# A decoder layer on one core: first pair's q and k projection at the head, p's projection beside the last retention pair, retention output as [tokens, d]

## The chip, the core and the metric

The kernel runs on one core of a Trainium2 chip. The core has TensorE (matrix products, PE in the profile, with its weight loads as PEld), VectorE (DVE), ScalarE (ACT), GpSimd (POOL) and SyncE (SP, which here only issues DMAs). ACT and POOL issue some DMAs too. Each engine takes its instructions in the order of the program that a scheduler has laid out at build time. The metric is device time in microseconds, median of several runs; lower is better.

## What is computed

One decoder layer on 512 tokens of width 2048, all in float32. Cut to what matters here:

```python
h = rms_norm(x, g_mix)
aq, ak, av, rq, rk, rv, rg = split(h @ w_in)                 # seven times 1024 columns
aq = rotate(rms_norm(aq per head, q_norm)); ak likewise      # 8 heads of 128
a_out = moba_attention(aq, ak, av)                           # 2 blocks of 256: plain causal attention here
r = retention(rotate(rq), rotate(rk) * 128**-0.5, rv)        # 8 heads, decay per head
r = r * rsqrt(mean(r * r, over the head) + 1e-6) * g_ret
r_out = silu(rg) * r
x += concat(a_out, r_out) @ w_o
x += (silu(rms_norm(x) @ w_gate) * (rms_norm(x) @ w_up)) @ w_down
x += (p @ w_ple_proj) * sigmoid(rms_norm(x) @ w_ple_gate + b)
```

`p` is a second input of 512 tokens by 256; its product with `w_ple_proj` depends on nothing else.

## The kernel before, in words

Every float32 operand is split into a high part H (float32r) and a low rest L, and a product is three passes: H·H, H·L, L·H (`mm3`, lines 62 to 64). `split` makes H with an ACT copy (line 54) and L with a DVE subtraction (line 55). A weight unit is 256 rows by 512 columns, 512 KB in one DMA on SP; its split is one ACT and one DVE instruction of 128x1024. All large products but the q and k projections go through a seven-product scheme (`Group`, products "1", "5", "6", "3", "7", "2", "4"): four quarters of a weight matrix are added on DVE (line 70), and sums of activation quarters, the factors, are kept as tiles s1, s5 and so on. PSUM banks of the scheme are X, Y and Z, two tiles each.

The program has these stages.

1. **Head.** Ten bf16 products on zeros; then four steps `Plain`, one for each 512 columns of `w_pp`: 24 products of p with a weight unit into `tp`, ACT copies, stores to DRAM (`ppd`). Beside them `first_factors` loads sixteen 128x512 chunks of transposed x on SP (line 428), scales them on ACT (line 429), splits them into `h`, and makes the factors s5, s6, s3, s7 from each pair of chunks. Then three groups of 336 products: the values of attention, the values of retention, and the gates. x is also read row by row for the sum of squares (lines 494 to 496).
2. **Gates.** `gates` applies silu, transposes the result with TensorE (32 transposes of 128x128, line 304), copies it on ACT and stores it as [d, tokens] in `sgd`.
3. **Head pairs.** Eight times: a pair of heads. `qk_attn(i)` (four attention pairs) or `qk_ret(i)` (four retention pairs) projects q and k of the pair: 8 weight units of 24 products into four PSUM tiles `acc`, 192 products. `attend` or `retain` then handles the two heads one after the other, and `factors` writes factors of the pair's output, through four buffers `o`, to DRAM (`s_mix`). In program order the projection of pair i+1 stands after the heads of pair i, and the scheduler interleaves the two. The evacuation of `qk_attn` takes DVE, ACT and POOL work for each of four token blocks before the next pair can use its `acc` tiles. The evacuation of `qk_ret` copies each `acc` tile to `zr`, swaps its halves with two DMAs on ACT's queue into `mr`, and multiplies with tables on DVE (lines 699 to 709); `zr` and `mr` share four buffers, so q of the two heads goes first and k waits for buffers.
4. **retain.** Scores of four key blocks (12 products), times decay on DVE, split into PH and PL; `weighted` gives o as [d, tokens] in 12 products with the values as the stationary operand. The norm over d runs over partitions: the squares are split, summed by a product with ones (`rms_of`, line 584), the diagonal is picked out on DVE, POOL takes the power, and `over_partitions` spreads the result with four transposes (line 85).
5. **Change to w_o.** When the last projection has read `h`, the tiles s1, s5, s6, s3 of the next stage take its place. `back` fills them from DRAM with DMAs on POOL's queue, pairs 0 to 5 first; the last pairs, and s7, s2, s4, follow. No projection is left beside the last pair.
6. **w_o, gate and up, down, ple gate.** Groups of the seven-product scheme to the end, untouched by the change.

Of the kernel before, what the change touches and what calls it, by code (L numbers as in the profile page):

```python
# [14 lines left out]
ALU = mybir.AluOpType  # L15
# [18 lines left out]
def layer_kernel(ctx, tc, x, xT, pT, g_mix, wqk, w_vg, qk_norm, g_ret, w_ow, g_ffn,  # L34
# [80 lines left out]
    sgd = dram.tile([P, 8, T], F32, name="sg")  # L115
# [266 lines left out]
    raws = []  # L382
    for k in range(2):
        raw = ev_tile("v", name="praw")
        nc.sync.dma_start(raw, pT[k * P:(k + 1) * P, :])
        raws.append(raw)
    pTH = []
    for k in range(2):
        pTH.append([ev_tile("e1" if k == 0 else "e5", name="pT", dt=F32R) for _ in range(2)])
        split(*pTH[k], raws[k])  # L390

    class Plain:

        def __init__(self, n):
            self.n = n
            self.raw = rawq.tile([P, 2, T], F32, name="raw", tag="c")
            nc.sync.dma_start(self.raw, w_pp[n])
            steps.append((self, "p", 0))
# [4 lines left out]
        def extract(self, p, u):  # L403
            self.wh = wq.tile([P, 2, T], F32R, name="wh", tag="wh")
            self.wl = wq.tile([P, 2, T], F32R, name="wl", tag="wl")
            split(self.wh, self.wl, self.raw)

        def multiply(self, p, u):
            for b in range(NB):
                o = tp_p.tile([P, T], F32, name="tp", tag="tp")  # L410
                at = slice(b * P, (b + 1) * P)
                for c in range(2):
                    mm3(o, pTH[c][0][:, at], pTH[c][1][:, at], self.wh[:, c, :], self.wl[:, c, :],
                        c == 0, c == 1)
                if b % 2 == 0:
                    t = rawq.tile([P, 2, T], F32, name="pp", tag="bd")
                nc.scalar.activation(t[:, b % 2], o, AF.Copy)
                nc.sync.dma_start(ppd[b][:, self.n], t[:, b % 2])

    for u in range(NS):  # L420
        Plain(u)

    def first_factors(k):

        a = []
        for c in (2 * k, 2 * k + 1):
            t = ev_tile("o", 4, name="x")
            nc.sync.dma_start(t, xT[c * P:(c + 1) * P, :])
            nc.scalar.activation(t, t, AF.Copy, scale=gm[:, c:c + 1])
            a.append(t)  # L430
        for c in range(2):
            split(h[:, 2 * k + c, 0, :], h[:, 2 * k + c, 1, :], a[c])
# [23 lines left out]
    def gates():  # L456
        got = {}

        def finish(th, nh, b, part, _):
            tb = 2 * th + b  # L460
            s = ev_tile("o", 4, name="sg") if (th, nh) == (0, 0) else part
            nc.scalar.activation(s, part, AF.Silu, scale=rstd[0][:, tb:tb + 1])
            got[tb, nh] = s
            if len([k for k in got if k[1] == nh]) == NB:
                def turn(k):
                    t = ev_tile("o", 4, name="A")
                    nc.scalar.activation(t, chunk_of(lambda b: got[b, nh], k), AF.Copy)
                    nc.sync.dma_start(sgd[:, 4 * nh + k], t)
                for k in range(4):
                    later(1 + k // 2, lambda k=k: turn(k))  # L470
# [4 lines left out]
    for u in range(4):  # L475
        groups[0].load("11", u)
# [6 lines left out]
    def beside(i):  # L483

        for k in {-2: [0], -1: [1], 0: [2, 3], 1: [4, 5], 2: [6], 3: [7]}.get(i, []):
            first_factors(k)
        if i == 4:
            for q in ("12", "22"):
                for u in range(4):
                    groups[0].load(q, u)  # L490
        if 4 <= i < 20:
            b, s = divmod(i - 4, NS)
# [4 lines left out]
        elif i == 20:  # L497
# [60 lines left out]
    ones = ap.tile([P, P], F32R, name="ones", tag="ones")  # L558
# [373 lines left out]
```

## Time and profile before

| | us |
|---|---|
| median of three runs | 2471.4 |
| lowest and highest run | 2466.14, 2471.67 |
| the profiled execution | 2465.03 |
| its span in the trace | 2463.3 |

The profile is of one execution. Its page gives the busy time of each engine, the span in 40 slices of 61.6 us, the chain of work that ended last, and the costliest groups of instructions. The trace answers finer questions: busy time and count of instructions in any stretch, an engine's instructions in order of time, and what each waited for. A busy TensorE is not a TensorE at its peak, since products are pipelined: the number of products in a stretch says more than the busy time.

### The profile page before, as it was taken

The page shows a single profiled execution, that of the slowest core. Times are in us where ns is not written, and L with a number is a line of the kernel's source. Part 1 is how long each engine was busy: PE and PEld are TensorE (multiplying, and loading weights), DVE is VectorE, ACT ScalarE, POOL GpSimd, SP SyncE. Part 2 cuts the span into 40 slices and gives each one's busy share as a digit, 9 for nine tenths or more (in the row PEclk, how much of TensorE's full clock was granted, in tenths as well). Part 3 has the DMA queues.
Part 4 walks back from the last instruction along what each step waited for, and adds up shares of the span by engine and source line. Part 5 has one row for each costly group of instructions (what it writes and reads, how often), then busy time and mean ns, then how long its engine had stood idle before and what let it go on. Part 6 is the DMA issues. An engine that isn't in the chain of part 4 may idle for free.

```text
span 2463.3 us, 29311 instructions
## 1 busy us (share of the span) xinstructions
PE 2347.9 (95%) x10454; PEld 1914.3 (78%) x10454; DVE 1965.7 (80%) x2624; ACT 1192.9 (48%) x1811; POOL 89.0 (4%) x77
## 2 busy tenths in 40 slices
PE   7899999998994999999999999999999999999898
PEld 5678888777773787788888888888877878888677
DVE  7788556776666799898889888898879787789897
ACT  7645434444332456455445554555444433446543
POOL 0000021220000100200000000000000000000000
PEclk8999999999996999999999999999999999999999
DMA  7544643335455569443564445543595676767763
GB/s 270 168 157 167 193 128 109 117 120 167 155 168 190 208 216 355 145 142 123 167 192 147 136 130 178 188 144 131 171 383 191 244 301 203 276 247 240 267 211 120
DMA packets 163667, 465.71 MB, mean 189 GB/s; under 512 B 18496, under 2 KB 27072, under 8 KB 158144
## 3 DMA queue, kind: packets, MB, share of 16 engines
q1 hardware_dynamic: 159184, 444.95, 53.4%
q0 software_dynamic: 1632, 14.68, 1.6%
q10 hardware_dynamic: 2704, 4.20, 0.7%
q8 instruction: 82, 1.34, 0.2%
q14 instruction: 65, 0.53, 0.1%
HBM read 353.14 MB, written 106.43 MB: 187 GB/s over the span
## 4 chain that ended last, share of the span: by engine, by line
PE 74%; DVE 11%; DMA 9%; issue 3%; ACT 3%; SPq 0%; POOL 0%; ACTq 0%; DVEq 0%; POOLq 0%
PE Y L62 8%; PE Y L63 8%; PE Y L64 8%; PE Z L63 6%; PE Z L64 6%; PE Z L62 5%; PE X L63 5%; PE X L64 5%; PE X L62 5%; PE acc L62 4%; PE acc L63 4%; PE acc L64 4%; DVE wl L55 4%; DVE raw L70 3%; DMA h<-o 2%
## 5 line engine op out<-in xcount | busy, mean ns | idle before, releaser
L54 ACT ACTIVATE wh<-raw 128x1024 fp32r<-128x1024 f32 x726 | 767.4, 1059 | 828.4 <-PE Y L64 274.1
L55 DVE TENSOR_TENSOR wl<-raw,wh 128x1024 fp32r<-128x1024 f32 x726 | 883.7, 1222 | 299.1 <-ACT wh L54 295.1
L70 DVE TENSOR_TENSOR raw<-raw 128x1024 f32<-128x1024 f32 x376 | 453.4, 1218 | 32.1 <-DMA raw<-in_w_gu 11.5
L63 PE MATMUL Y<-wl,s 128*128 128x512 f32 x1080 | 425.6, 394 | 3.7 <-DVE wl L55 3.6
L64 PE MATMUL Y<-wh,s 128*128 128x512 f32 x1080 | 421.6, 390 | 0.0
L62 PE MATMUL Y<-wh,s 128*128 128x512 f32 x1080 | 379.0, 391 | 10.0 <-ACT wh L54 10.0
L63 PE MATMUL Z<-wl,s 128*128 128x512 f32 x752 | 297.6, 396 | 5.3 <-DVE wl L55 5.3
L64 PE MATMUL Z<-wh,s 128*128 128x512 f32 x752 | 293.7, 391 | 0.8 <-DVE s L55 0.8
L62 PE MATMUL Z<-wh,s 128*128 128x512 f32 x752 | 266.5, 394 | 3.1 <-DMA s<-h 2.2
L63 PE MATMUL X<-wl,s 128*128 128x512 f32 x656 | 258.3, 394 | 4.7 <-DVE wl L55 4.5
L64 PE MATMUL X<-wh,s 128*128 128x512 f32 x656 | 256.6, 391 | 0.0
L62 PEld LDWEIGHTS Y<-wh,s 128*128 128x128 f32 x1080 | 201.9, 188 | 56.9 <-ACT wh L54 15.2
L63 PEld LDWEIGHTS Y<-wl,s 128*128 128x128 f32 x1080 | 203.2, 188 | 49.3 <-DVE wl L55 8.0
L64 PEld LDWEIGHTS Y<-wh,s 128*128 128x128 f32 x1080 | 203.2, 188 | 41.0
L62 PE MATMUL X<-wh,s 128*128 128x512 f32 x656 | 231.6, 393 | 3.6 <-ACT wh L54 3.6
L63 PEld LDWEIGHTS Z<-wl,s 128*128 128x128 f32 x752 | 142.2, 189 | 38.5 <-DVE wl L55 9.6
L62 PEld LDWEIGHTS Z<-wh,s 128*128 128x128 f32 x752 | 141.0, 189 | 34.0 <-ACT wh L54 2.5
L64 PEld LDWEIGHTS Z<-wh,s 128*128 128x128 f32 x752 | 142.1, 189 | 29.6 <-DVE s L55 1.2
L63 PEld LDWEIGHTS X<-wl,s 128*128 128x128 f32 x656 | 123.8, 189 | 34.0 <-DVE wl L55 8.3
L62 PEld LDWEIGHTS X<-wh,s 128*128 128x128 f32 x656 | 123.3, 189 | 31.8 <-ACT wh L54 6.2
L64 PEld LDWEIGHTS X<-wh,s 128*128 128x128 f32 x656 | 123.9, 189 | 25.5
L62 PE MATMUL acc<-h,wh 128*128 128x512 f32 x256 | 101.9, 398 | 6.2 <-ACT zr L699 5.4
(200 smaller groups left out, 2844.1 us busy)
## 6 DMA issues: line engine op xcount, KB each, us to landing
raw<-in_w_gu SPq DMA_DIRECT2D x176, 512.0 KB, 4.3
raw<-in_w_dn SPq DMA_DIRECT2D x88, 512.0 KB, 5.8
a<-o SPq DMA_DIRECT2D x154, 256.0 KB, 2.8
raw<-in_wqk SPq DMA_DIRECT2D x64, 512.0 KB, 3.5
s<-a SPq DMA_DIRECT2D x14, 2048.0 KB, 11.0
raw<-in_w_vg SPq DMA_DIRECT2D x48, 512.0 KB, 5.1
raw<-in_w_ow SPq DMA_DIRECT2D x32, 512.0 KB, 5.6
xin<-x SPq DMA_DIRECT2D x64, 256.0 KB, 5.8
```

The source lines that it names most:

```text
L54: nc.scalar.activation(H, src, AF.Copy)
L55: nc.vector.tensor_tensor(L, src, H.bitcast(F32), op=ALU.subtract)
L62: nc.tensor.matmul(o, aH, bH, start=start, stop=False, skip_group_check=goes_on)
L63: nc.tensor.matmul(o, aH, bL, start=False, stop=False, skip_group_check=goes_on)
L64: nc.tensor.matmul(o, aL, bH, start=False, stop=stop, skip_group_check=goes_on)
L70: nc.vector.tensor_tensor(o, a, b, op=ALU.add)
```

## The change

First, `Plain` is now the q and k projection of attention pair 0: eight steps of 24 products that read `h` straight from its chunks into the banks Y and Z; the result goes to DRAM (`zd`) and is loaded back as `z0` when the pair's evacuation runs. `first_factors` is made in a second pass that loads x's chunks again. Second, p's projection stands after the last head pair. Third, the gates stay [tokens, d]: no transposes. Fourth, `retain` makes o as [tokens, d] with PH and PL as the stationary operand and the two parts of the values side by side as 256 columns, 20 products; the norm is then along the free axis, and the result is turned by four transposes at the end. Fifth, `back` is issued on SP, in pieces of two pairs, at the start of the last pair, and that pair's factors for "1", "5", "6", "3" go straight into the tiles.

```diff
     class Plain:
-        def __init__(self, n):
-            self.n = n
-            self.raw = rawq.tile([P, 2, T], F32, name="raw", tag="c")
-            nc.sync.dma_start(self.raw, w_pp[n])
-            steps.append((self, "p", 0))
+        def __init__(self):
+            self.raw, self.w = {}, {}
+            steps.extend((self, "q", u) for u in range(NC // 2))
+
+        def load(self, u):
+            self.raw[u] = rawq.tile([P, 2, T], F32, name="raw", tag="l1" if u < 4 else "c")
+            nc.sync.dma_start(self.raw[u], wqk[0, u])
...
         def multiply(self, p, u):
+            if u == 0:
+                self.acc = [pools["chain"].tile([P, T], F32, name=k, tag=k) for k in ("Y0", "Y1", "Z0", "Z1")]
+            wh, wl = self.w.pop(u)
             for b in range(NB):
-                o = tp_p.tile([P, T], F32, name="tp", tag="tp")
                 at = slice(b * P, (b + 1) * P)
                 for c in range(2):
-                    mm3(o, pTH[c][0][:, at], pTH[c][1][:, at], self.wh[:, c, :], self.wl[:, c, :],
-                        c == 0, c == 1)
...
+                    k = 2 * u + c
+                    mm3(self.acc[b], h[:, k, 0, at], h[:, k, 1, at], wh[:, c, :], wl[:, c, :], k == 0, k == NC - 1)
+            if u == NC // 2 - 1:
+                later(1, self.evac)
+
+        def evac(self):
+            for b in range(NB):
+                t = ev_tile("o", 4, name="z0")
+                nc.scalar.activation(t, self.acc[b], AF.Copy)
+                nc.sync.dma_start(zd[b], t)
...
     def beside(i):
-        for k in {-2: [0], -1: [1], 0: [2, 3], 1: [4, 5], 2: [6], 3: [7]}.get(i, []):
-            first_factors(k)
...
+        if -2 <= i < NC // 2 - 2:
+            for k in (2 * i + 4, 2 * i + 5):
+                t = h_chunk(k)
+                split(h[:, k, 0, :], h[:, k, 1, :], t)
+            first.load(i + 2)
+        if 3 <= i < 3 + NC // 2:
+            first_factors(i - 3)
...
+        if i == 0:
+            for b in range(NB):
+                t = rm_tile("z0")
+                nc.sync.dma_start(t, zd[b])
+                evac(b, t)
+        else:
+            rows([wqk[i, u] for u in range(NC // 2)], evac)
...
-        o = weighted(v, (PH, PL), j)
+        hd = slice(j * HD, (j + 1) * HD)
+        r = rp_tile("r", (P, NB, HD))
+        ms = stat.tile([P, NB], F32, name="ms")
+        for half in range(2):
+            o = at_p.tile([P, 2, 2, HD], F32, name="at", tag="at")
+            for qb in (2 * half, 2 * half + 1):
+                for kb in range(qb + 1):
+                    at = slice(384 * kb + qb * P, 384 * kb + (qb + 1) * P)
+                    nc.tensor.matmul(o[:, qb % 2], PH[:, at], v[:, kb, :, hd], start=kb == 0, stop=False)
+                    nc.tensor.matmul(o[:, qb % 2], PL[:, at], v[:, kb, :, hd], start=False, stop=kb == qb)
+            both = slice(2 * half, 2 * half + 2)
+            nc.scalar.activation(r[:, both], o[:, :, 0], AF.Copy)
+            plus(r[:, both], r[:, both], o[:, :, 1])
...
+        for qb in range(NB):
+            nc.scalar.activation(sq[:, qb * P:(qb + 1) * P], r[:, qb], AF.Square, accum_out=ms[:, qb:qb + 1])
+        nc.vector.tensor_scalar(ms, ms, 1.0 / HD, EPS, op0=ALU.mult, op1=ALU.add)
         rs = stat.tile([P, NB], F32, name="rs")
-        rms_of(sq, [rm_tile("sqs", dt=F32R) for _ in range(2)], sq, HD, rs)
-        nc.vector.tensor_tensor(r, over_partitions(rs), r, op=ALU.mult)
-        return r
+        power(rs, ms, NB)
...
     def back(p, pairs):
-        nc.gpsimd.dma_start(s_o[p][:, pairs].bitcast(F32), s_mix[p][:, pairs].bitcast(F32))
+        nc.sync.dma_start(s_o[p][:, pairs].bitcast(F32), s_mix[p][:, pairs].bitcast(F32))
...
+        if i + 1 == 2 * NPAIR:
+            h_ctx.close()
...
+            for u in range(3):
+                for p in "156":
+                    back(p, slice(2 * u, 2 * u + 2))
+            for p in "156":
+                back(p, slice(6, 7))
+            back("3", slice(0, 7))
...
+    for k in range(2):
+        raw = rm_tile("praw")
+        nc.sync.dma_start(raw, pT[k * P:(k + 1) * P, :])
+        both = ap.tile([P, 2, T], F32R, name="pT", tag="rope" if k == 0 else "pT")
...
+    for n in range(NS):
+        wh, wl = weights(w_pp[n])
+        accs = [acc_p.tile([P, T], F32, name="acc", tag="acc") for _ in range(NB)]
```

The order that the scheduler makes of it differs at three places. On SP at the start of the program, before:

```order
L385 DMA praw<-in_pT 128x512 x2
L397 DMA raw<-in_w_pp 128x1024 x4
L204 DMA raw<-in_w_vg 128x1024 x4
L478 DMA ident<-in_ident_c 128x128
```

and now (in_xT is transposed x, in_wqk the weights of q and k, in_w_vg those of values and gates):

```order
L422 DMA x<-in_xT 128x512 x2
L390 DMA raw<-in_wqk 128x1024
L422 DMA x<-in_xT 128x512
L390 DMA raw<-in_wqk 128x1024 x3
L422 DMA x<-in_xT 128x512
L390 DMA raw<-in_wqk 128x1024 x2
L422 DMA x<-in_xT 128x512
L204 DMA raw<-in_w_vg 128x1024
L422 DMA x<-in_xT 128x512
L204 DMA raw<-in_w_vg 128x1024 x3
L422 DMA x<-in_xT 128x512
```

Chunks of x, weights of q and k, and weights of the values now alternate, and the twelve weight units of the first group stand among the chunks that the projection needs.

On PE at the end of the projection of attention pair 1, which in both programs is followed by that of pair 2 (`acc`; `at` with qkH are scores, `at` with PH are the weighted values, `tp` with pt and z are transposes). Before:

```order
L64 MATMUL acc<-wh,h 128x512
L62 MATMUL at<-qkH 128x256 x2
L63 MATMUL at<-qkL,qkH 128x256
L64 MATMUL at<-qkH,qkL 128x256
L63 MATMUL at<-qkL,qkH 128x256
L64 MATMUL at<-qkH,qkL 128x256
L62 MATMUL acc<-wh,h 128x512
```

and now:

```order
L64 MATMUL acc<-wh,h 128x512
L665 MATMUL tp<-ident,pt 128x128 x7
L62 MATMUL at<-PH,v 128x512
L640 MATMUL tp<-ident,z 128x128 x4
L63 MATMUL at<-PL,v 128x512
L64 MATMUL at<-PH,v 128x512
L62 MATMUL at<-PH,v 128x384
L63 MATMUL at<-PL,v 128x384
L64 MATMUL at<-PH,v 128x384
L62 MATMUL at<-PH,v 128x256
```

The projection ends earlier against the attention of pair 0: the last transposes and the weighted values of its first head now stand behind it, with no product of a projection between them.

On PE around the last retention pair (line 738 turns the output of the pair before; the scores of four key blocks, 12 products, and the 20 products of lines 722 and 723 of the first head stand between the two pieces shown). Before, after the last projection product:

```order
L584 MATMUL tp<-sqs,ones 128x512 x2
L85 MATMUL tp<-ident,rs 128x128 x4
L62 MATMUL at<-qkH 128x512
L63 MATMUL at<-qkL,qkH 128x512
L62 MATMUL at<-qkH 128x384
```

and now:

```order
L738 MATMUL tp<-ident,r 128x128 x4
L62 MATMUL at<-qkH 128x512
L63 MATMUL at<-qkL,qkH 128x512
L62 MATMUL at<-qkH 128x384
```

```order
L64 MATMUL at<-qkH,qkL 128x512
L62 MATMUL acc<-wh,pT 128x512
L63 MATMUL acc<-wl,pT 128x512
L62 MATMUL acc<-wh,pT 128x512
L63 MATMUL acc<-wl,pT 128x512
```

p's 96 products stand behind the first head's scores and weighted values and the first scores of the second head; none stands ahead of them.

The reload, before, on POOL's queue (s are the tiles of the next stage, 3072 columns are 1.5 MB):

```order
L747 DMA s_6454<-mix_86 128x3072
L747 DMA s_6455<-mix_87 128x3072
L747 DMA s_6456<-mix_88 128x3072
L747 DMA s_6457<-mix_89 128x3072
L747 DMA s_6454<-mix_86 128x512
```

and now on SP's, from the last of the first ten pieces on:

```order
L746 DMA s_6346<-mix_86 128x512
L204 DMA raw<-in_w_ow 128x1024
L176 DMA mix_87<-o 128x512
L176 DMA mix_88<-o 128x512
L176 DMA mix_89<-o 128x512
L176 DMA mix_90<-o 128x512
L746 DMA s_6347<-mix_87 128x512
L176 DMA mix_91<-o 128x512
L746 DMA s_6348<-mix_88 128x512
L176 DMA mix_92<-o 128x512
L746 DMA s_6349<-mix_89 128x3584
L778 DMA praw<-in_pT 128x512 x2
```

Nine pieces of 512 KB and one of 256 KB stand ahead of the stores of the factors (`mix<-o`), and the load of p stands behind all of it.

## Rows read from the trace of the kernel before

**Rows 1.** The page: busy time by engine, then TensorE and its granted clock in 40 slices.

```profile
PE 2347.9 (95%) x10454; PEld 1914.3 (78%) x10454; DVE 1965.7 (80%) x2624; ACT 1192.9 (48%) x1811; POOL 89.0 (4%) x77
...
PE   7899999998994999999999999999999999999898
...
PEclk8999999999996999999999999999999999999999
```

**Rows 2.** Stretches: length, busy time (instructions) by engine, granted clock, DMA share, GB/s.

```profile
0.00:40.00 40.00, 33.78 (x124) 23.37 (x124) 22.12 (x39) 29.94 (x51) 0.20 (x4) 0.96 0.97 345
40.00:80.00 40.00, 28.49 (x86) 19.62 (x87) 39.50 (x68) 25.00 (x48) 0.00 (x0) 0.79 0.31 98
80.00:160.00 80.00, 75.11 (x320) 59.08 (x320) 60.78 (x67) 46.11 (x74) 1.39 (x1) 1.00 0.61 207
160.00:220.00 60.00, 60.00 (x266) 49.69 (x265) 46.47 (x48) 29.56 (x32) 0.00 (x0) 1.00 0.60 195
440.00:460.00 20.00, 16.76 (x77) 13.27 (x76) 15.36 (x31) 9.30 (x43) 7.35 (x8) 0.91 0.20 67
760.00:780.00 20.00, 1.62 (x5) 0.90 (x5) 10.08 (x19) 2.81 (x6) 1.03 (x1) 0.51 1.01 362
780.00:800.00 20.00, 7.29 (x20) 5.83 (x21) 10.69 (x20) 5.37 (x11) 1.15 (x2) 0.50 0.45 153
800.00:820.00 20.00, 16.71 (x71) 13.61 (x71) 12.73 (x21) 7.61 (x13) 1.64 (x2) 0.88 0.27 79
```

**Rows 3.** TensorE in order of time: start, duration, line, tiles [idle before, releaser].

```profile
755.12 0.40 PE L64 MATMUL acc<-h,wl 128*128 128x512 f32 x1
...
791.39 0.80 PE L62 MATMUL at<-qkH 128*128 128x512 f32 x1 [26.34 <-ACT qkH L54]
...
801.44 0.28 PE L63 MATMUL at<-PL,v 128*128 128x256 f32 x1
801.56 0.28 PE L64 MATMUL at<-PH,v 128*128 128x256 f32 x1
...
811.84 0.39 PE L62 MATMUL X<-wh,s 128*128 128x512 f32 x1
```

**Rows 4.** The other engines there: POOL's reload, DVE on a swap, ACT on a store.

```profile
755.84 2.94 POOL L747 DMA_DIRECT2D s<-mix  x5 [6.93 <-PE at L64]
...
776.22 0.69 DVE L705 TENSOR_TENSOR zr<-zr,ropeT 128x512 f32<-128x512 f32 x1 [4.04 <-DMA mr<-zr]
...
782.79 0.42 ACT L54 ACTIVATE o<-r 128x256 fp32r<-128x256 f32 x1 [9.94 <-DMA mix<-o]
```

**Rows 5.** The chain of waits, start and length: an earlier swap, four transposes, the store.

```profile
643.05 6.17 DMA mr<-zr
...
753.44 0.44 PE tp L85 x4
...
767.18 15.25 DMA mix<-o
```

**Rows 6.** Groups of instructions, 0 to 160 us: count, busy us, mean ns, idle before.

```profile
L55 DVE TENSOR_TENSOR wl<-raw,wh 128x1024 fp32r<-128x1024 f32 x41 | 49.9, 1219 | 23.6 <-ACT wh L54 23.4
L54 ACT ACTIVATE wh<-raw 128x1024 fp32r<-128x1024 f32 x41 | 42.7, 1051 | 11.5 <-PE Z L64 5.3 <-PE X L64 2.8 <-DMA raw<-in_w_pp 2.2
...
L429 ACT ACTIVATE x<-x,gm 128x512 f32<-128x512 f32 x16 | 11.3, 715 | 5.0 <-DMA x<-in_xT 4.9
L55 DVE TENSOR_TENSOR h<-x,h 128x512 fp32r<-128x512 f32 x16 | 10.9, 682 | 0.0
...
L54 ACT ACTIVATE h<-x 128x512 fp32r<-128x512 f32 x16 | 9.9, 624 | 0.2
...
L67 DVE TENSOR_TENSOR t<-x,t 128x256 f32<-128x256 f32 x24 | 9.4, 417 | 0.1
```

**Rows 7.** SP's waits in 0 to 160 us: total, times, longest.

```profile
SPq L428 <- DVE t L67: 28.7, 8, 12.2
```

**Rows 8.** TensorE's waits in 600 to 760 us: total, times, longest.

```profile
PE tp L584 <- ACT sqs L54: 6.5, 3, 2.3
```

More of the change, by code (lines that the diff above doesn't have):

```diff
@@ L462, in finish @@
             nc.scalar.activation(s, part, AF.Silu, scale=rstd[0][:, tb:tb + 1])
[L463 to L470, printed above, removed]
+            later(1, lambda: nc.sync.dma_start(sgd[:, tb, nh * T:(nh + 1) * T], s))
         return evacuate(finish)
@@ L496, in beside @@
             nc.scalar.activation(sq, t, AF.Square, accum_out=ssq[0][:, b, s:s + 1])
-        elif i == 20:
+        elif i == 22:
             rstd_of(ssq[0], rstd[0])
@@ L577, in load_ropeT @@
         tab[0] = t
-    def rms_of(src, parts, tmp, n, r):
-        split(*parts, src)
-        st = tp_p.tile([P, NB, P], F32, name="tp", tag="tp")
-        for k, part in enumerate(parts):
-            nc.tensor.matmul(st.rearrange("p b t -> p (b t)"), ones, part, start=k == 0, stop=k == 1)
-        d = tmp.rearrange("p (b t) -> p b t", b=NB)
-        nc.vector.tensor_tensor(d, st, ident[:, None, :].to_broadcast([P, NB, P]), op=ALU.mult)
-        nc.vector.tensor_reduce(r, d, axis=AX.X, op=ALU.add)
-        nc.vector.tensor_scalar(r, r, 1.0 / n, EPS, op0=ALU.mult, op1=ALU.add)
-        power(r, r, NB)
     def qk_pair():
@@ L600, in v_of @@
             nc.sync.dma_start(v[:, b].bitcast(F32), vd[i // NPAIR][:, b, :, j * 256:(j + 1) * 256].bitcast(F32))
-        return [v[:, b, 0] for b in range(NB)], [v[:, b, 1] for b in range(NB)]
+        return v
     def p_tiles():
@@ L649, in evac @@
             made.append(z)
-        rows([wqk[i, u] for u in range(NC // 2)], evac)
+        if i == 0:
[5 more added lines that the diff above has]
+            rows([wqk[i, u] for u in range(NC // 2)], evac)
         return made
@@ L754, in layer_kernel @@
             made = [retain(qk, v, j, 2 * (i - NPAIR) + j) for j in range(2)]
-        factors(*made, spill(s_mix, i, 0))
+        spilled = spill(s_mix, i, 0)
+        direct = into(s_o, i)
+        factors(*made, lambda p: (direct if p in s_o else spilled)(p))
         if i + 1 < 2 * NPAIR:
@@ L774, in layer_kernel @@
     s_o.update({p: factor_tile(p) for p in "724"})
-    for part in (slice(6, 7), slice(7, 8)):
-        for p in "156":
-            back(p, part)
-    back("3", slice(6, 8))
     for p in "724":
```

90 lines of the change are left out of this document (40 added, 50 removed).

## The prediction

> **What bounds the kernel now.** I read the page first: TensorE is busy for 95% of the span, and only one slice of the 40, the 13th, shows a low share and a low granted clock [rows 1]. So a gain is a stretch in which TensorE issues no products, or fewer products; other engines matter where TensorE waits for them. Next I counted products by stretch. Undisturbed, 266 products take 60.00 us, 0.2256 us each [rows 2]. I call lost whatever a stretch takes beyond its count times its price. In the head, 0 to 160 us, there are 124 + 86 + 320 products, ten of them warm-ups [rows 2]: 520 x 0.2256 = 117.3, so 42.7 us are lost. Between the last projection product (start 755.12) and the first w_o product (811.84) lie 56.5 us [rows 3] with 5 + 20 products in the first 40 us at half the clock (0.51, 0.50, and 0.88 with 71 products in the next 20 us) [rows 2]. These two places hold nearly all that this change can win. The chain of waits names the second: a store of a factor, 15.25 us [rows 5], under a reload of some 4.9 MB that moves 362 GB/s with the DMA engines full [rows 2, 4]. The first scores wait 26.34 us there for the split of the rotated q [rows 3], which hangs on a swap beside the same reload [rows 4].
>
> The profiled execution took 2465.03 us, the median is 2471.4. I sum against the profiled one and place the result between the two. About 0.3%, 7.4 us, is what a measurement of this kernel can tell from no change.
>
> **The change part by part.**
>
> 1. **Head.** p's 96 products (21.7 us) go to the end of the pairs, 192 of q and k (43.3 us) come from the pairs; that is work moved, and the term is the change of the lost time. First product: two chunks of x and a unit of weights, 1 MB at 345 GB/s, 3.0 us; then scale and split of two chunks on ACT, 2 x (0.715 + 0.624), and of the weights, 1.051, then 1.219 on DVE [rows 2, 6]: 8 us, with some 1.5 for the first issue 9.5. On SP twelve units of group "1" are mixed in, so that the chunk for unit 3 of the projection is the 27th transfer, behind 9.5 MiB: 29 us at 345 GB/s, 32.4 with its steps, against 9.5 + 84 x 0.2256 = 28.4 for the product: 4 us of wait. SP itself can hold: it stood 28.7 us behind factor steps that must free an x buffer [rows 7], and each chunk now comes twice. DVE then has, up to the fifth factor pair that "5" needs after 270 products, 16 splits of h at 0.682, 15 of weights and 11 sums at 1.219, and 45 short steps at 0.417 [rows 6]: 61.4 us, which starts only as data lands and ends at 78 to 82 us. TensorE comes there at 9.5 + 4 + 60.9 = 74: a wait of some 8 us, taken high because DVE was already full in 40 to 80 us (39.50 of 40) [rows 2]. After such a wait products run at half clock (0.50 in 780 to 800 [rows 2]); 15 of them cost 3.4. With 3 for small gaps 28 us are lost instead of 42.7: **-15**. Bounds: -25 (no DVE wait, no late chunk) and -3 (both twice as long, SP held as before). ACT's second scaling, 16 x 0.715 = 11.4 us, fits: ACT was busy 29.94 of 40 us at most [rows 2]. The ACT copies of the result into DRAM and its load wait for nobody.
> 2. **Gates.** 32 transposes of 0.11 us (four in 0.44 [rows 5]): **-3.5**. They stood on TensorE's path; the ACT copies behind them did not.
> 3. **retain.** 20 products of 256 columns at 0.12 [rows 3] are 2.4 us a head, against 12 products with 4224 columns, 1.9, and two products with ones, 0.45. So TensorE gains no work. The waits for the squares (6.5 us in three in that stretch [rows 8], two of them in the pairs) go; the four new transposes may wait for the new norm, ACT, DVE and POOL steps in a row, up to the same. **-2**, bounds -5 and +4. ACT gets about 2 us a head more, four squares with accumulation; its load there leaves room.
> 4. **Attention.** The projection of pair 1 now ends ahead of the first head's tail, where no projection product is left to fill. The nearest row is such a boundary of before: 440 to 460 us, 77 products, 20 - 17.4 lost there with the clock at 0.91 [rows 2], and as much around it: **+5**, bounds 0 and +6.
> 5. **Change to w_o.** In the order on SP ten pieces, 4.9 MB, stand ahead of the stores and p's load: 13 to 14 us at 362 GB/s [rows 2]. The swaps stay on ACT's queue. Alone a swap took 6.17 us [rows 5], beside the reload DVE waited until 776.22 for one [rows 4]. I keep the 36 us from the last projection product to the first scores, as the reload is as large. p's 96 products stand behind the scores and outputs of the first head, some 11 us later by order, so none of them fills the first 36 us. They and the second head take 27.6 us; the first w_o product comes 36 + 11 + 27.6 = 75 us after the last projection product, against 56.5: +18.5, of which 21.7 is p's work taken out of the head. **-3**, bounds -13 and +10. The DVE rotations stand ahead of the factor sums in the order, and the store that ended the chain [rows 4, 5] is mostly replaced by factors written in place, so p's products cover the rest.
> 6. **z0.** The load of the first pair's projection and its norm may hold the transposes of pair 0: **+1**, bounds 0 and +5.
>
> The sum is -15 - 3.5 - 2 + 5 - 3 + 1 = -17.5: 2447.5 on the profiled execution, 2453.9 on the median. I forecast 2450.
>
> The reload's move from POOL to SP I cost at nothing in term 5, since the same bytes pass 1.01 of the DMA engines' time in 760 to 780 us [rows 2]. The Trainium skill (DMA: Bandwidth & Descriptors, Issuing engines are not separate DMA queues) says that DMAs of any issuing engine end on the same 16 engines and interleave; by that the 36 us stay, and the row agrees as far as one stretch can.
>
> **The rivals.**
>
> - **B, the swaps come free.** The 1.5 MB pieces on POOL's queue become 0.5 MB on SP's; a swap then takes the 6.17 us it took alone [rows 5], and the scores start at 27 instead of 36 us: -9, 2441. For it: the reload delays swaps now and SP has a single queue. Against: the bytes are the same. The Trainium skill (DMA: Bandwidth & Descriptors, Queues, rings and completion order) has each DMA engine take turns between queues, a packet at a time; by that a swap would share with the reload whichever queue it has, which speaks for the forecast, and no run here shows the turns.
> - **C, the head stays bound.** SP, blocked at x buffers as in [rows 7], brings weights and chunks in the wrong order, or DVE is full from the start; the change then doesn't do what it says, the lost time moves from before the first product to the first 90 us, and saves 3 instead of 15: 2462. For it: DVE full [rows 2], each chunk loaded twice. Against: DVE was at 22.12 of 40 in the first stretch [rows 2], so there is room ahead of the crowd.
> - **D, slower, by SP's queue at the last pair.** The second pair of swaps, the stores, p's load and p's weights all stand behind or beside the reload on SP: a second round of swaps beside it (+6), stores and p 14 us behind ten pieces (+14), p's split and copies on ACT and DVE behind that (+5), and half clock throughout, 45 more half steps (+10): +35, 2485. It decides where the first w_o product starts over 100 us after the last projection product. For it: 15.25 us for one store [rows 5]. Against: p's load has 47 us until its product is due, and ten pieces need 14.
>
> **How the numbers follow.** Forecast (2440 to 2460) 0.52, B 0.13, C 0.17, D 0.12, anything else 0.06. Faster by over 0.3% means under 2464: 0.47 of the forecast's chance, all of B's, 0.10 of C's and 0.03 of the rest, 0.73. Slower is D, 0.12; the remainder, 0.15, lies within. The range leaves out D, the lower tail of B and half of the rest: 2434 to 2470.
>
> **What would show it.** Count in 0 to 160 us: (160 - 28) / 0.2256 = 585 products without warm-ups, 533 by C, 631 at the other bound. DVE near full and a lower clock in 60 to 85 us show term 1's wait; SP's waits, its cause. No wait at the products with ones, and short ones at the new transposes, show term 3. A new stall where projection 1 ends shows term 4. Two lengths show term 5: last projection product to first scores (36; B 27), and to the first w_o product (75; B 66; D over 100). I would be wrong if the second length is far off, or if pairs other than these change their gaps.

## The result, and the profile after

| | before | after |
|---|---|---|
| median us | 2469.3 (four runs, 2466.14 to 2471.67) | 2448.56 (four runs, 2446.12 to 2450.52) |
| ratio | | 0.9916, 95% interval 0.9899 to 0.9934 |
| span of the profiled execution | 2463.3 | 2446.4 |

The changed kernel is 0.84% faster, 20.7 us; the forecast was 2450. The total came out as forecast. Its parts did not.

The page of the changed kernel, TensorE by busy time, in 40 slices, and its granted clock, against [rows 1]:

```profile
PE 2332.6 (95%) x10470; PEld 1911.5 (78%) x10470; DVE 1958.1 (80%) x2632; ACT 1211.8 (50%) x1886; POOL 62.4 (3%) x63
...
PE   8799999998986998999999999999999999999898
...
PEclk9899999999997999999999999999999999999999
```

The deep slice is still the 13th, now a 6 and not a 4, and the 12th ahead of it is an 8, since the last projection ends 29 us sooner; the second slice, 61 to 122 us, is a 7 with the clock at 8 tenths.

The head of the changed kernel by stretches: length, busy time (instructions) of PE, PEld, DVE, ACT, POOL, granted clock, DMA share, GB/s, against [rows 2]:

```profile
0.00:40.00 40.00, 31.93 (x115) 23.45 (x116) 14.96 (x19) 21.64 (x30) 0.20 (x4) 0.96 0.88 331
40.00:80.00 40.00, 30.81 (x136) 25.18 (x135) 36.46 (x59) 29.49 (x53) 0.00 (x0) 0.94 0.43 132
80.00:160.00 80.00, 71.11 (x297) 57.42 (x298) 58.34 (x81) 48.95 (x85) 1.92 (x1) 0.92 0.65 217
```

Without the ten warm-ups that is 115 + 136 + 297 - 10 = 538 products where there were 520. 18 x 0.2256 = 4.1 us were won in the head, not 15. TensorE's waits in 0 to 160 us (waiting operation, what it waited for, total, times, longest) name where the rest went:

```profile
PE Z L62 <- ACT z L414: 16.4, 1, 16.4
PE Y L62 <- ACT wh L54: 5.3, 2, 4.8
PE Y L62 <- ACT h L54: 2.0, 1, 2.0
```

The 4.8 us lie ahead of the first product, at 10.50 us; the 2.0 us are the wait for a late chunk of x, at 33.51. The loss is the one wait of 16.4 us. The products of group "5" need bank Z, and Z still held the projection's result. TensorE in order of time at that place, then ACT (start, duration, instruction, in brackets the idle time before and its end):

```profile
70.42 0.39 PE L64 MATMUL X<-wh,h 128*128 128x512 f32 x1
87.17 0.80 PE L62 MATMUL Z<-wh,s 128*128 128x512 f32 x1 [16.36 <-ACT z L414]
```

```profile
84.96 0.40 ACT L54 ACTIVATE s<-t 128x256 fp32r<-128x256 f32 x1
85.27 1.06 ACT L414 ACTIVATE z<-Y 128x512 f32<-128x512 f32 x2
86.22 0.41 ACT L54 ACTIVATE s<-t 128x256 fp32r<-128x256 f32 x1
86.53 0.59 ACT L414 ACTIVATE z<-Z 128x512 f32<-128x512 f32 x1
```

The projection's last product started at 62.04; the copies that free its banks ran at 85 to 88 us, among the factor steps (`s<-t`). Behind the wait the first dozen products come 0.43 us apart and not 0.23; the granted clock in 80 to 90 us is 0.50.

Now the change to w_o. The changed kernel's TensorE there (last projection product, first scores, first product of p, first w_o product), against [rows 3]:

```profile
726.16 0.39 PE L64 MATMUL acc<-h,wl 128*128 128x512 f32 x1
...
751.92 0.80 PE L62 MATMUL at<-qkH 128*128 128x512 f32 x1 [24.93 <-ACT qkH L54]
...
762.48 0.40 PE L62 MATMUL acc<-wh,pT 128*128 128x512 f32 x1
...
789.34 0.40 PE L62 MATMUL X<-wh,s 128*128 128x512 f32 x1
```

From the end of the last projection product (start plus 0.23) the scores come at 25.5 us (36.0 before) and the first w_o product at 63.0 (56.5 before). p's 21.7 us lie in those 63.0, so without them this stretch is 15.2 us shorter: 10.5 of them ahead of the scores, 4.7 behind.

A table holds the whole profiled difference. T0 is the end of the last projection product, S the first scores after it, X the first w_o product; times in us, of the profiled execution of each kernel. "Short retain alone" and "change without it" are two of the experiments below.

| | 0 to T0 | T0 to S | T0 to X | X to end |
|---|---|---|---|---|
| before | 755.3 | 36.0 | 56.5 | 1651.5 |
| after | 726.4 | 25.5 | 63.0 | 1657.1 |
| short retain alone | 750.8 | 24.5 | 40.3 | 1657.7 |
| change without it | 748.3 | 31.4 | 79.2 | 1650.5 |

Up to T0 the change takes off 29.0, of which 21.7 are p's products, moved: 7.3 won. T0 to X: +6.5, with p's 21.7 moved in: 15.2 won. X to the end: 5.6 lost. 7.3 + 15.2 - 5.6 = 16.9, the difference of the spans. The last column falls in two: 1650.5 and 1651.5 with the old retain, 1657.1 and 1657.7 with the short one.

### The profile page after: what moved, and what is told of

Same layout as the page of the kernel before. It is cut to its first block, busy times and chain, and to the rows that moved or that the text cites. A ratio compares the mean times of both kernels' runs of the same rounds, so it can differ in the third digit from the quotient of the medians.

```text
span 2446.4 us, 29405 instructions
## 1 busy us (share of the span) xinstructions
PE 2332.6 (95%) x10470; PEld 1911.5 (78%) x10470; DVE 1958.1 (80%) x2632; ACT 1211.8 (50%) x1886; POOL 62.4 (3%) x63
## 4 chain that ended last, share of the span: by engine, by line
PE 67%; DVE 10%; DMA 6%; issue 3%; ACT 1%; ACTq 0%; POOL 0%; SPq 0%; DVEq 0%
PE Y L63 8%; PE Y L64 8%; PE Y L62 8%; PE Z L63 5%; PE Z L64 5%; PE Z L62 5%; PE X L63 5%; PE X L64 5%; PE X L62 5%; PE acc L62 4%; PE acc L64 4%; PE acc L63 3%; DVE wl L55 3%; DVE raw L70 2%; DMA mr<-zr 1%
## 5 line engine op out<-in xcount | busy, mean ns | idle before, releaser
L62 PE MATMUL Z<-wh,s 128*128 128x512 f32 x752 | 267.4, 395 | 19.6 <-ACT z L414 16.4
L62 PEld LDWEIGHTS Z<-wh,s 128*128 128x128 f32 x752 | 141.5, 190 | 50.5 <-ACT z L414 16.8
```

The lines of the kernel that those rows point to most:

```text
L62: nc.tensor.matmul(o, aH, bH, start=start, stop=False, skip_group_check=goes_on)
```

## The experiments

Each ratio below is to runs of the kernel before on the same chip. Where the intervals of two ratios overlap, the times alone do not tell the two kernels apart, and what is said of a few us between them rests on the profiles, one execution of each kernel.

**1. The reload on POOL's queue again.** The changed kernel, one word.

```diff
-        nc.sync.dma_start(s_o[p][:, pairs].bitcast(F32), s_mix[p][:, pairs].bitcast(F32))
+        nc.gpsimd.dma_start(s_o[p][:, pairs].bitcast(F32), s_mix[p][:, pairs].bitcast(F32))
```

> The changed kernel with the reload (back) issued on POOL's queue again, same pieces. In the changed kernel the first scores come 25.5 us after the last projection product (36.0 in the kernel before) and the first w_o product 63.0 us after it (56.5 before). Theory: the gain comes from the q swaps being issued before the reload, because the retention head's tail no longer stands ahead of the evacuations on ACT; the queue of the reload does not matter, so 25.5 stays within 3 us and the time within 4 us of 2448.6. Rival B of the prediction: it is SP's queue with smaller pieces that frees the swaps; then the first scores go back to about 36 us and the time rises by about 10 us.

Measured: 2445.57 us, ratio 0.9918 (0.9900 to 0.9935). S 23.5, X 63.2 us after T0. The queue does not bring the 36 us back, so SP's queue, rival B's cause, falls. B's smaller pieces are in both of these kernels, and this run does not test them. The Trainium skill (DMA: Bandwidth & Descriptors, Issuing engines are not separate DMA queues) says that the issuing engine does not change which 16 engines move the data; the two runs agree, 23.5 against 25.5 us.

**2. The short retain alone.** The kernel before with the changed `gates`, `v_of` and `retain`, nothing else.

```diff
+        for half in range(2):
+            o = at_p.tile([P, 2, 2, HD], F32, name="at", tag="at")
...
-        rms_of(sq, [rm_tile("sqs", dt=F32R) for _ in range(2)], sq, HD, rs)
-        nc.vector.tensor_tensor(r, over_partitions(rs), r, op=ALU.mult)
-        return r
+        power(rs, ms, NB)
```

> The kernel before with one part of the change alone: the gates stay as [tokens, d] and retain makes its output as [tokens, d] with the short norm; head, reload and p's projection as before. Theory: the squares, the products with ones and the spread of the norm no longer stand ahead of the evacuations, so the q swaps are issued ahead of the reload and the first scores come about 26 us after the last projection product instead of 36; with 3.5 us of transposes gone at the gates and about 5 us less waiting in the retention pairs the time is about 2452 (-17). Rival: the order does not matter beside the reload, the first scores stay at 36 us, and the change is worth its own terms alone, 3.5 + 2 to 5 us: about 2462.

Measured: 2449.24 us, ratio 0.9919 (0.9898 to 0.9940). This part alone gives what the whole change gives. Its TensorE at the change to w_o (last projection product, the turned output, the scores):

```profile
750.57 0.39 PE L64 MATMUL acc<-h,wl 128*128 128x512 f32 x1
754.23 1.12 PE L733 MATMUL tp<-ident,r 128*128 128x128 f32 x4 [3.28 <-DVE r L729]
775.33 0.80 PE L62 MATMUL at<-qkH 128*128 128x512 f32 x1 [19.98 <-ACT qkH L54]
```

The reason is in the order of issue. First ACT in the kernel before, then ACT and POOL with the short retain (the q copies out of PSUM, the swap DMAs, the reload):

```profile
757.85 0.60 ACT L699 ACTIVATE zr<-acc 128x512 f32<-128x512 f32 x1
758.48 0.47 ACTq L702 DMA_DIRECT2D mr<-zr  x1
758.98 0.88 ACTq L703 DMA_DIRECT2D mr<-zr  x1
760.06 0.60 ACT L699 ACTIVATE zr<-acc 128x512 f32<-128x512 f32 x1 [1.62 <-DVE sqs L55]
760.69 0.47 ACTq L702 DMA_DIRECT2D mr<-zr  x1
```

```profile
747.58 0.48 ACTq L678 DMA_DIRECT2D mr<-zr  x1
748.10 0.61 ACTq L679 DMA_DIRECT2D mr<-zr  x1
...
750.83 0.47 ACTq L678 DMA_DIRECT2D mr<-zr  x1
751.34 0.61 ACTq L679 DMA_DIRECT2D mr<-zr  x1
```

```profile
751.28 2.91 POOL L741 DMA_DIRECT2D s<-mix  x5 [0.47 <-DMA mr<-zr]
```

Before, the reload was issued at 755.84 [rows 4] and the q swaps 2.6 to 5.4 us behind it, because the last head's squares stood ahead of the copies on ACT (the second copy waited for `sqs`). With the short norm three of the four swaps go out 0.5 to 3.7 us ahead of the reload and the last one with it. The changed kernel has this order too; its first two swaps left at 723.14 and 723.70, then:

```profile
724.99 0.47 ACTq L683 DMA_DIRECT2D mr<-zr  x1
725.50 0.61 ACTq L684 DMA_DIRECT2D mr<-zr  x1
```

```profile
726.59 8.58 SPq L746 DMA_DIRECT2D s<-mix  x10
```

A second delay stands beside this one. In the kernel before, k's copies stood on ACT until 783.11 us, behind the split of a factor that waited 9.94 us for a store [rows 4], and that store was under way beside the reload as well [rows 5]. With the short retain the first k copy ran at 757.27, ahead of such a wait.

**3. The order alone.** The kernel before, long tail and all, with the first four DMAs of the reload held back until q is rotated.

```diff
             for p in "1563":
+                nc.vector.tensor_scalar(s_o[p][:, 0, 0, :2], qk[1][0][:, :2].bitcast(F32), 0.0, None, op0=ALU.mult)
                 back(p, slice(0, 6))
```

> The kernel before with one edit: four tiny DVE writes, fed by the rotated q of the last pair's second head, hold the first four DMAs of the reload back until both q swaps have landed; the retention head's long tail stays. Before, the q swaps were issued 2.6 to 5.4 us after the reload and took up to 15.0 us; the first scores came 36.0 us after the last projection product. In the run with the short tail alone the q swaps were issued ahead of the reload, and the scores came at 24.5. Theory: the order of swap and reload is the larger part of those 11.5 us; the q swaps land in 4 to 7 us, k's now meet the reload instead, and the scores come at 27 to 31 us; time 5 to 9 us below the kernel before. Rival: the tail itself (squares, ones, spread of the norm, factors on ACT and DVE ahead of the rotation) sets it; scores stay at 34 us or later and the time within 3 us of the kernel before.

Measured: 2460.62 us over ten runs, ratio 0.9978 (0.9968 to 0.9989). S 20.6 us after T0, less than expected. The swap tile's landing times from 700 us on, the kernel before and then this run (issue to landing, minimum, median, maximum):

```profile
DMA to landing us min/median/max: 2.2/3.8/15.0
```

```profile
DMA to landing us min/median/max: 2.2/2.4/10.7
```

and its reload and TensorE:

```profile
768.35 2.17 POOL L747 DMA_DIRECT2D s<-mix  x4 [3.82 <-DVE s L766]
```

```profile
764.59 1.11 PE L85 MATMUL tp<-ident,rs 128*128 128x128 f32 x4 [6.94 <-POOL rs L73]
772.78 0.80 PE L62 MATMUL at<-qkH 128*128 128x512 f32 x1 [7.08 <-ACT qkH L54]
```

So with the swaps ahead of the reload even the long tail gives 20.6 us, 15.4 less than before; the short tail brought 11.5. Here k's last swaps leave at the reload's start, and the last, issued at 769.29, is the one of 10.7 us. Only some 6 us reach the end: the first w_o product stands 50.2 us after T0, 6.3 less than before. The four large pieces of the reload start 16.2 us after T0 instead of 0.5, and the four transposes wait 6.94 us for the head's norm: POOL's power waits there for DVE (`rs`), where the rotations now stand ahead of it. Which of these holds the first w_o product was not separated. That the reload, issued ahead, is the cause of the long wait for the scores is shown, and that the tail's own steps cost little there follows. This run frees the swaps and the stores of the factors from the reload together, so it does not say how much of the wait belongs to each.

**4. The change without the short retain.** The changed kernel with the old `gates`, `retain` and norm.

```diff
-        power(rs, ms, NB)
...
+        rms_of(sq, [rm_tile("sqs", dt=F32R) for _ in range(2)], sq, HD, rs)
+        nc.vector.tensor_tensor(r, over_partitions(rs), r, op=ALU.mult)
```

> The changed kernel with the old gates (transposed) and the old retain: what is left is the first pair's projection at the head, p's projection at the last pair and the reload on SP in pieces. Theory: by difference from the run with the short retain alone (2449 against 2449 for the whole change) these parts are worth nothing together: the head's lost time falls by 4 us, the attention pairs lose 5 more, and p's products add to the last pair what they take out of the head; the first scores come 33 to 38 us after the last projection product again; time 2464 to 2470. Rival: the pieces on SP shorten the swaps by themselves; the scores stay under 29 us and the time is about 2456.

Measured: 2481.64 us, ratio 1.0056 (1.0036 to 1.0075): slower than the kernel before by some 14 us, which no theory had. By the table, 0 to T0 is 7.0 shorter with 21.7 of p moved out, so 14.7 longer by itself; T0 to X takes 79.2, 1.0 more than before without p's 21.7; the rest is 1.0 shorter. The scores come 31.4 us after T0, between the theory's 33 to 38 and the rival's 29. So the old retain costs 33 us beside the other parts and 18 alone. TensorE's waits in the retention pairs of this run, 575 to 748 us:

```profile
PE acc L62 <- ACT zr L704: 4.7, 2, 2.7
PE tp L85 <- POOL rs L73: 2.6, 1, 2.6
PE tp L583 <- ACT sqs L54: 2.2, 1, 2.2
```

I summed what the spacing of TensorE's starts has beyond the undisturbed price of each shape, from the projection of the second pair (in the kernel before, of the first) to the first retention projection, and from there to T0. The first stretch loses 12.0 us before, 16.9 in the changed kernel and 23.0 here, the second 23.5, 17.7 and 29.9. At the change to w_o, the reload on SP went out at 748.47 while the swaps of q followed at 751.84 to 759.54: the old order again. Yet these swaps landed in 6.4 to 7.4 us, where those of the kernel before took 8.7 to 15.0, so rival B's shorter swaps do come with the smaller pieces; what was late was their issue, spread over 7.7 us. Of the 10.5 us that the change takes off the wait for the scores, 4.6 are there with the old order. Why both stretches lose more than before is not settled: the waits named are the old ones, and the granted clock around them is lower (0.91 in 680 to 720 us).

**5. Own buffers for the first pair's result.** The changed kernel.

```diff
-                t = ev_tile("o", 4, name="z0")
+                t = ev_tile("e1" if b < 2 else "e5", name="z0")
```

> The changed kernel with one edit: the four tiles that take the first pair's projection out of PSUM have buffers e1 and e5 (two each, idle there) instead of the four buffers o that x's chunks rotate through. In the changed kernel TensorE waits 16.4 us for the copies that free bank Z; the copies ended at 88.2 us though their products ended at 62.3. Theory: the copies stood on ACT behind the chunks' steps only for their buffer; with their own they run at 63 us, and TensorE goes on until DVE's list holds it at about 85 us: the wait falls to 4 to 10 us and the time by 6 to 12 us, to about 2440. Rival (term 1 of the prediction: DVE's list is the bound): TensorE waits for the factors of group 5 as long, another releaser stands at the same place, and the time stays within 3 us.

Measured: 2444.0 us, ratio 0.9913 (0.9897 to 0.9929). The copies run at once, the last starting at 61.27 where it started at 87.61, the wait for them is gone, and the head by stretches is:

```profile
61.27 0.61 ACT L414 ACTIVATE z<-Z 128x512 f32<-128x512 f32 x1
```

```profile
0.00:40.00 40.00, 32.80 (x127) 24.21 (x128) 16.14 (x20) 23.78 (x34) 0.20 (x4) 1.00 0.89 334
40.00:80.00 40.00, 35.59 (x155) 28.43 (x153) 38.07 (x60) 31.90 (x57) 0.00 (x0) 0.98 0.48 155
80.00:160.00 80.00, 73.88 (x302) 56.94 (x303) 62.13 (x85) 48.15 (x82) 1.92 (x1) 0.97 0.67 217
```

127 + 155 + 302 - 10 = 574 products, 36 more than the changed kernel: 8.1 us. T0 comes 5.2 us sooner (721.2); the two stretches behind, summed as in experiment 4, lose 18.9 and 18.3 us instead of 16.9 and 17.7. The buffer was the cause of the 16.4 us; the rival that DVE's list holds TensorE just as long falls. The median is 4.6 us lower, less than the theory's 6 to 12, and by the ratios it is not told apart from the changed kernel's.

**6. p's products in the gap.** The changed kernel; p is split into `PH` and `PL` ahead of the last pair, its products go through the transposition banks, the results are staged in the tiles of s6 and s3.

```diff
+            pH, pL = p_tiles()
+            for k in range(2):
+                split(pH[:, k * T:(k + 1) * T], pL[:, k * T:(k + 1) * T], pr[:, k])
+            for n in range(NS):
+                wh, wl = weights(w_pp[n])
+                for b in range(NB):
+                    acc = tp_p.tile([P, T], F32, name="tp", tag="tp")
...
+                    t = stage[n // 2][:, 4 * (n % 2) + b]
+                    nc.scalar.activation(t, acc, AF.Copy)
```

> The changed kernel with p's projection moved ahead of the last pair's scores: p is loaded a pair earlier and split into the tiles PH and PL, the 96 products go through the two transposition banks, the results are staged in the tiles s6 and s3 before their reload. Theory: TensorE is idle there for 25 us for want of the rotated q, so the 21.7 us of products fit in; first scores stay at 25 to 30 us after the last projection product, the first w_o product comes at 42 to 47 instead of 63, and the time falls by 14 to 20 us, to about 2431. Rival: the stores of p's result (4 MB, 11 to 12 us at 362 GB/s) delay the reload of s6 and s3 behind them, and swaps beside them, so that the first w_o products wait: only -5, about 2443.

Measured: 2439.71 us, ratio 0.9889 (0.9874 to 0.9904). S 30.3, X 52.6 us after T0: 10.4 us of p's 21.7 are hidden. Half of the theory holds: the gap takes products, but with two banks TensorE waits for the copies (5.4 us in four waits), ACT stands at the swaps, and the scores come 4.8 us later. X is 5.6 us or more behind the theory's 42 to 47, and the time, 8.9 us lower by the medians, lies between the theory's 14 to 20 and the rival's 5. Whether p's stores delayed anything, as the rival has it, is not shown.

**7. zr in buffers of its own.** The changed kernel; k's copies no longer share four buffers with q's.

```diff
-            z = rm_tile("zr")
+            z = rp_tile("zr")
```

> The changed kernel with one edit: zr takes the four buffers rp, so that the evacuations of k need not wait for q's rotation (in the changed kernel k's copies came 10.1 and 14.1 us after the last projection product, its swaps were issued at 12 to 20 us, and the scores came at 25.5). Theory: the second round of swaps is what is left of the wait; issued with q's, k's swaps land beside the reload within 7 to 10 us and the scores come at 16 to 20 us; time 5 to 8 us below 2448.6. Rival: eight swap transfers at once beside the reload share what two rounds shared, and ACT, which issues them, stands longer at each; scores at 23 to 26 us and the time within 2 us.

Measured: 2437.56 us, ratio 0.9882 (0.9860 to 0.9903), by one word 11 us below the changed kernel by the medians, 8 by the ratios. k's copies stand at 1.2 us after T0 and not 10.1; S 15.8, X 51.7.

```profile
724.51 1.08 ACT L680 ACTIVATE zr<-acc 128x512 f32<-128x512 f32 x2
727.53 0.47 ACTq L683 DMA_DIRECT2D mr<-zr  x1
```

```profile
723.06 0.39 PE L64 MATMUL acc<-h,wl 128*128 128x512 f32 x1
739.12 0.79 PE L62 MATMUL at<-qkH 128*128 128x512 f32 x1 [15.23 <-ACT qkH L54]
```

The second round of swaps was 9.7 of the 25.5 us; 15.8 are left. The rival, that the swaps at once share what two rounds shared, falls.

**8. Residual sums on POOL in the w_o stage.** The changed kernel loses time after X too; this was the test of DVE as its cause.

```diff
-            plus(o, part, t)
+            (plus if i or (th, nh) == (0, 0) else lambda o, a, b: nc.gpsimd.tensor_tensor(o, a, b, op=ALU.add))(o, part, t)
```

> The changed kernel with one edit in the w_o stage: 12 of its 16 residual sums of 128x512 (0.686 us each on DVE, 8.2 us together) run on POOL, which is idle there. In the first 200 us from the first w_o product TensorE loses 16.8 us in the changed kernel, 18.0 with the short retain alone, 10.3 in the kernel before, at products that wait for weight splits. Theory: the shorter gap ahead of that stage leaves DVE less time to get ahead with sums and splits of weights, and DVE is the bound there; with 8 us taken off it the loss falls by 4 to 8 us and the time as much. Rival: ACT's split or the weights' DMA is the bound, or POOL slows DVE down; loss and time within 2 us of the changed kernel.

Measured: 2452.49 us, ratio 0.9938 (0.9921 to 0.9955), 4 us above the changed kernel by the medians, with intervals that overlap; the loss in the first 200 us from X is 17.5 against 16.8. TensorE's waits in 789 to 989 us, the changed kernel and then this one:

```profile
PE Y L62 <- ACT wh L54: 2.7, 2, 1.4
PE Z L63 <- DVE wl L55: 2.3, 2, 1.4
PE tp L304 <- DVE e L70: 2.0, 2, 1.1
```

```profile
PE Y L62 <- ACT wh L54: 3.7, 2, 2.4
PE tp L304 <- POOL e L333: 2.4, 2, 1.6
PE Y L63 <- DVE wl L55: 1.1, 1, 1.1
```

The theory falls: the waits for DVE shrink, those for ACT's split and for POOL's sums take their place. What costs 5.6 us after X stays open. It comes with the short retain: that alone shows it too (6.2), and the change without it does not (1.0 less than before).

**9. Together.** Edits 5, 6 and 7; then with the reload on POOL; then with its first tiles held back as well.

> The changed kernel with three edits together: p's products ahead of the last pair's scores (alone 2439.7, scores at 30.3 us, first w_o product at 52.6 us after the last projection product), own buffers for the first pair's result in the head (alone 2444.0), and a new one: zr takes the four buffers rp, so that zr and mr no longer share four and k's swaps need not wait for q's rotation. Theory: gains of different stages add, and k's swaps are issued with q's: scores at 20 to 25 us, first w_o product at 44 to 48; 2439.7 - 4.5 - 5 = 2430. Rival: four swaps beside the reload and p's stores take as much longer as they start earlier; scores stay at 29 to 31 and the time is about 2435.

> The three edits of p_gap_z0_rp (2431.8) with the reload on POOL's queue. With the reload on SP, ACT stood up to 7.1 us at the issue of a swap while pieces of the reload were under way; with the reload on POOL alone it did not (swaps of k issued within 2.7 us of each other, scores at 23.5 instead of 25.5, 2445.6 instead of 2448.6). Theory: the same gain here, 2 to 5 us, and p's stores, which wait on SP behind the reload, come earlier, so that p's products pause less: 2426 to 2430. Rival: within 2 us of 2431.8.

> best_pool with the reload of the first two tiles held back, by two tiny DVE writes, until the second head's q is rotated. Theory: the swaps land in 2 to 5 us as in the run with the late reload (scores there at 20.6 us), p's products fill those 20 us, and the reload of 1 and 5 is done 14 us later, when the scores of the first head are under way: first w_o product at 42 to 46 us after the last projection product against 58 with the reload on SP; 2420 to 2428. Rival: the reload, started 10 us later and on a queue where POOL's powers wait behind it, is what the first w_o products wait for: first w_o product at 50 us or later, time as best_pool or above.

Measured: 2431.75 us, ratio 0.9856 (0.9841 to 0.9870); 2428.05 us, 0.9844 (0.9821 to 0.9867); 2428.66 us, 0.9845 (0.9825 to 0.9865). S, X: 23.5, 58.3; 21.3, 53.4; 18.6, 51.1. The first is short of its theory: with p in the gap and zr in its own buffers X comes 58.3 us after T0, later than with either edit alone, so their gains do not add. With the reload on POOL the median is 3.7 us lower, where its theory had it, though the two intervals overlap. Holding the reload brings the scores sooner and the end no further, as its rival had it. The version with the reload on POOL beats the kernel before by 1.56% and the changed kernel by some 18 to 20 us.

## Why the prediction was right, and which of its steps failed

The sum said -17.5 on the profiled execution; it is -16.9. That they agree is luck: the sum has 7.2 us too much gain up to T0 and 12.2 too little behind it, and lacks the 5.6 lost after X.

- **Up to T0** terms 1, 2, 3, 4 and 6 said -15 - 3.5 - 2 + 5 + 1 = -14.5; measured -7.3. Term 1 failed at one sentence: "The ACT copies of the result into DRAM and its load wait for nobody." TensorE waited 16.4 us for them, since their tiles rotate with x's chunks. Its numbers ahead of that were near: the first product came at 10.5 us (9.5), and the late chunk cost 2.0 us (4). And with that wait taken away (experiment 5) the head issues 574 products where the term had 585. The wait for DVE's list was put in its place by the prediction with 8 us, half the size. So rival C gave the head's gain nearly (3, measured 4.1), by luck too, since its reason was another.
- **Term 4** held: the attention stretch loses 16.9 instead of 12.0 us, +4.9 for +5; in the other profiles, by such a sum, it loses 10 to 13 us without that part of the change and 16 to 23 with it. **Term 3** held in sign: waits at the products with ones are gone, and from the first retention projection to T0 the short retain alone takes 238.1 us where the kernel before takes 241.2, near the -2. In the changed kernel this stretch takes 236.0 and loses 17.7 instead of 23.5 us, so part of that gain needs the other parts, and how is open. Terms 2 and 6 were not measured apart; ACT waited 4.2 us for z0's load, TensorE 0.5 us at the transposes there.
- **T0 to X**, term 5, said -3, measured -15.2; the first w_o product came at 63.0 us and not at 75, which the prediction had named as a sign of being wrong. The step that failed is "I keep the 36 us ..., as the reload is as large." The order was not the old one: the short norm, which the prediction costed at the retention heads alone, takes the last head's squares off ACT ahead of q's copies, so the swaps leave ahead of the reload. Experiments 2 and 3 show it. The size was not the old one either: the prediction read 4.9 MB for the reload of before, which issued four pieces of 1.5 MB and one of 256 KB, almost a third more than the ten pieces that now stand ahead of the stores. But the short retain alone keeps the old pieces and has its scores at 24.5 us. Scores came at 25.5 us, near rival B's 27, but by the order, which B did not have; SP's queue had no part in it (experiment 1), the smaller pieces may have (experiment 4). From the scores to X the changed kernel takes 37.5 us, the short retain alone 15.8: the difference, 21.7, is p's work in full. That p's products fill none of the gap held. The store that the term calls mostly replaced still stands there for the pair before: its last split on ACT, at 748.78 us, waited for one.
- **After X** the prediction had nothing; 5.6 us were lost there, with the short retain, cause open.
- **Rival D** did not come, X at 63 and not over 100 us. But the side it stood for is real: without the short retain the rest of the change is 14 us slower than before (experiment 4), mostly ahead of T0 and not at SP's queue.

The forecast's number was right, and only in part for its reasons: by the runs, the short retain carries the change; the moves of the two projections and the reload on SP together bring nothing on balance beside it, and cost without it. No run has one of the two moves alone.

## What to carry to other kernels

When work is taken off an engine's queue, look at what stands behind it there, DMA issues above all: here a shorter norm, costed at 2 us, took 16.2 us off the change to w_o, mostly because small transfers on the path left ahead of a large one. A copy that frees a PSUM bank is on the path of whoever needs the bank next, and a tile that it shares with a slower rotation delays it: before calling it covered, name its buffer and the bank's next user. A sum that comes out right is no proof of its terms; putting the short retain alone into the kernel before, and taking it alone out of the changed one, showed which part carried the gain.

## What the runs showed of the hardware

- A swap of 128 KB landed in 2.2 to 6.2 us in the retention pairs of the kernel before that have no reload beside them; the prediction's 6.17 is near the longest. At the change to w_o it landed in 3.6 to 7.6 us in the changed kernel, ahead of the reload or among its pieces of 512 KB, and in 8.7 to 15.0 us in the kernel before, issued 2.6 to 5.4 us behind the first of four pieces of 1.5 MB. The Trainium skill (DMA: Bandwidth & Descriptors, Queues, rings and completion order) has each DMA engine take turns between queues by packets; no run shows the turns. Behind pieces of 512 KB swaps took 6.4 to 7.4 us with the reload on SP (experiment 4) and 5.9 to 7.6 with it on POOL (experiment 1); behind pieces of 1.5 MB on POOL they took 7.2 to 9.7 with the short retain alone. So the size of the pieces, or the bytes ahead, counted for more than the queue; the two were not separated.
- With the reload on SP, ACT stood at the issue of a swap: in the changed kernel at 742.59 and 746.09, 3.5 us apart, and its next instruction came 7.11 us after the one before. With the reload on POOL the four were issued in 2.6 us. The cause is in the program. The swaps and SP's transfers share one small set of completion semaphores, and the trace has each of the delayed issues end with the landing of the piece of the reload that had the swap's semaphore last; POOL's transfers have semaphores of their own. In the change without the short retain it shows at a split of the rotated q, which reads nothing of the reload and still waits for it behind a swap:

```profile
769.35 0.47 ACTq L708 DMA_DIRECT2D mr<-zr  x1
769.86 0.63 ACT L54 ACTIVATE qkH<-zr 128x512 fp32r<-128x512 f32 x1 [4.30 <-DMA s<-mix]
```

Which engine issues the large transfer mattered to the issue of small ones more than to their travel.
